# Eleven loads of V issued by GpSimd instead of SyncE, in a cross-covariance attention kernel

## Chip, cores and metric

One core of one Trainium2 chip. The metric is device time in microseconds (us) for one execution of the whole kernel. Beside it stands one execution taken by the hardware profiler; its span runs from the first to the last instruction. The engines are named as in the profile: PE is TensorE (PEld its weight loads), DVE is VectorE, ACT is ScalarE, POOL is GpSimd, SP is SyncE. SPq and POOLq are the instruction streams of SP and POOL that issue DMAs. The 16 DMA engines move the data, whoever issues.

## The reference

```python
batch, heads, seq, dim = 8, 12, 512, 64          # Q, K, V: float32
Q_norm = Q / (np.linalg.norm(Q, axis=-2, keepdims=True) + 1e-10)
K_norm = K / (np.linalg.norm(K, axis=-2, keepdims=True) + 1e-10)
attn = np.einsum('bhnd,bhne->bhde', Q_norm, K_norm)
attn = np.exp(attn - np.max(attn, axis=-1, keepdims=True))
attn = attn / (np.sum(attn, axis=-1, keepdims=True) + 1e-10)
return np.einsum('bhnd,bhde->bhne', V, attn).astype(np.float32)
```

For each of the 96 heads the attention matrix is 64 x 64, over the feature dimension. Each of Q, K, V and the output is 12.58 MB, so 50.3 MB cross the DMA engines.

## The kernel before

**Tiles.** Four heads make a unit `u` (24 of them), two units a stage `s` (12), two stages a group `w` (6). A stage has 1 MB of Q and 1 MB of K; both live in one tile `qk32[s]`, of which there are three buffers. V is loaded per group in two tiles `v32[w, r]` of 1 MB (128 partitions, 8 KB each in one piece), of which there are three buffers too, so the load of one V tile waits until the tile three before it has been read. Q, K and the output go in pieces of 4 KB. Early stages and the last one load Q and K in halves of 512 KB, and the last V tile comes in two halves.

**Work.** For each unit, Q is cast to bf16 by POOL and K by DVE or ACT (`cast_qk`, L212, named cq), DVE makes two masked copies of K (`mask_k`, L222, named mk), ACT squares Q (`square_q`, L228), and PE multiplies (`grams`, L245, and `norms_q`, L253). For each stage there follow the sums and powers that give the norms, the scaling of the 64 x 64 matrices on POOL (`scale_k`, L293, tile kqs), their transposes, the exponentials on ACT (L307) and the normalised bf16 matrix on DVE (L316). V is cast to bf16 (`cast_v`, named cv, tile vb), each half of a tile on POOL or ACT, transposed by PE (L327), copied out of PSUM by ACT (tile vt) and multiplied with the attention matrix (`outs`, L343). DVE copies the result to the output tile `so` (`ocopy`, four copies a stage), and two stores of 512 KB a stage take it to memory. All casts and copies go through one helper and so stand under L172 (ACT), L174 (DVE) or L176 (POOL).

**Order.** The order of instructions is written out by a planner (`Order`). It gives each piece an engine, the pieces it comes after, and a rank, and simulates the pieces with fixed costs; the list of pieces sorted by their planned begin is then emitted, each piece into the instruction stream of its engine, which executes in that order. The loads and stores are pieces of one planned engine, DMA. Which real engine issues a load is decided only in the function that emits it (`load_qk`, `load_v`, `store`); in the kernel before, that is SP for all but the first two loads of K, which ACT issues. A load's place among the other instructions of the issuing engine is that of the planned list. Around the first V loads the list reads, in this order: Q cast of unit 2 (POOL), first V load, Q cast of unit 3 (POOL), second V load, loads of Q and K of stage 4, Q cast of unit 4 and scaling of stage 0 (POOL), third V load, Q cast of unit 5 (POOL). The fourth stands behind POOL's cast of the first V tile, the fifth behind POOL's cast of the second one.

The line that calls the load and gives its waits is L453 in the loop over `w` and `r`: `free` are the casts of the V tile three before, and `last` keeps the V loads in order. Only the last tile is asked for in halves; all eleven others are whole (`c is None`).

Of the kernel before, what the change touches and what calls it, by code (L numbers as in the profile page):

```python
# [111 lines left out]
def kernel(  # L112
# [7 lines left out]
    nc = tc.nc  # L120
# [16 lines left out]
    Vu = V.rearrange("b h (p t) d -> (b h p) (t d)", t=2 * T).rearrange("(w r p) x -> w r p x", r=2, p=128)  # L137
# [55 lines left out]
    def load_v(w, r, c):  # L193
        if (w, r) not in v32:
            v32[w, r] = vp.tile([128, 2, T * D], F32, name="v32")
        o, i = v32[w, r], Vu[w, r].rearrange("p (c x) -> p c x", c=2)
        if c is None:
            nc.sync.dma_start(out=o.rearrange("p c x -> p (c x)"), in_=Vu[w, r])
        else:
            nc.sync.dma_start(out=o[:, c], in_=i[:, c])  # L200

# [220 lines left out]
    for u in range(U):  # L422
        s, r = divmod(u, 2)
# [23 lines left out]
    for w in range(W):  # L447
        for r in range(2):
            halves = (0, 1) if (w, r) == (W - 1, 1) else (None,)
            n = 2 * w + r - NB["v"]  # L450
            for c in halves:
                free = [("cv", n // 2, n % 2, h) for h in range(2)] if n >= 0 else []
                piece(("lv", w, r, c), {"DMA": X if c is not None else 2 * X}, free, [last], v_at(4 * w + 2 * r + (c or 0)), load_v, w, r, c)  # L453
                last = ("lv", w, r, c)
            for c in range(2):
                free = [("vt", w - NB["vb"], *t) for t in turns(w - NB["vb"])] if w >= NB["vb"] else []
                piece(("cv", w, r, c), {"POOL": 1.04, "DVE": (0.62, BIAS["cv"]), "ACT": (0.95, BIAS["ca"])},
                      [("lv", w, r, c if len(halves) == 2 else None)] + free, [("cv", w, r, 0)] if c else [], R["cv"] + 0.01 * (4 * w + 2 * r + c), cast_v, w, r, c)
        for n, (q, f) in enumerate(turns(w)):
            if f is None:  # L460
                before = turns(w)[n - 1] if n else turns(w - 1)[-1] if w else None
                wait = [("vc", w if n else w - 1, *before)] if before else []
            else:
                wait = [("kq", S - 1), ("rd", S - 1)] + ([("vc", w, *turns(w)[n - 4])] if n >= 4 and turns(w)[n - 4][1] is not None else [])
            piece(("vt", w, q, f), {"PE": 0.4 if f is not None else 0.65}, [("cv", w, r, c) for r in range(2) for c in range(2)] + wait, [turned],
                  R["vt"] + 0.02 * w, vtrans, w, q, f)
            turned = ("vt", w, q, f)
            copies = {"ACT": 0.57 if f is not None else 0.97}
            copies["DVE"] = (0.6 if f is not None else 1.12, BIAS["vc"])
            free = [("ou", 2 * (w - NB["vt"]) + e, x) for e in range(2) for x in range(4)] if w >= NB["vt"] else []  # L470
            piece(("vc", w, q, f), copies, [("vt", w, q, f)] + free, [("vc", w, *turns(w)[n - 1])] if n else [], R["vc"] + 0.02 * w, vcopy, w, q, f)
# [57 lines left out]
```

## Time and profile before

| | |
|---|---|
| time, median of 3 runs | 127.59 us (127.54 to 127.77) |
| the profiled execution's span | 125.9 us |
| bytes moved, mean rate over the span | 50.63 MB, 402 GB/s |
| busy: PE | 79.6 us (63%) |
| busy: DVE | 98.8 us (78%) |
| busy: ACT | 91.0 us (72%) |
| busy: POOL | 50.0 us (40%) |
| V loads issued by SP | 11 of 1024 KB, 2 of 512 KB |
| POOL's waits for V to land | 8.2 us, 6 times |
| SP's waits for ACT's cast of V before a V load | 9.9 us, 3 times |
| PE's waits for the masked K (gram matmuls) | 23.3 us, 18 times |

The profiler's page shows each engine's busy time, the span in 40 equal slices with the busy share in tenths, the DMA queues with packets, bytes and share, and groups of instructions by line. Answers of the trace give the same for a stretch of time (busy time by stage), the instructions of one engine in order (timeline: start, length, engine, line, operation, output and input, and in brackets the idle time before with what ended it), and the waits. Queue q1 is the one that SP's DMAs use, q10 that of ACT, q8 the fetching of instructions. A DMA on 16 engines is recorded as packets; their start, length, queue and size are in the trace.

### The profile page before, as it was taken

The numbers are of one execution on the slowest core, as the hardware profiler recorded it, in microseconds if no ns is written. First come the engines' busy times: TensorE is split into PE (matmuls) and PEld (weight loads), VectorE is DVE, ScalarE is ACT, GpSimd is POOL, SyncE is SP. The second block draws the span as 40 slices with busy tenths as digits, with TensorE's granted clock in tenths as the row PEclk, the third lists the DMA queues.
The fourth block names the chain that finished last, engine by engine and source line by source line (L and its number), as shares of the span: only waits on it lengthen the run. The fifth ranks groups of instructions, "written<-read, shape, count | busy, mean of one in ns | idle before, by whom it ended". The sixth has DMA issues, their size and how long they took to land.

```text
span 125.9 us, 4630 instructions
## 1 busy us (share of the span) xinstructions
PE 79.6 (63%) x1944; PEld 63.9 (51%) x1944; DVE 98.8 (78%) x198; ACT 91.0 (72%) x217; POOL 50.0 (40%) x68
## 2 busy tenths in 40 slices
PE   0036949258789857766776668676794875976000
PEld 0035848236668745555665555555683764754000
DVE  3189676967959399987999989999979999999200
ACT  4243476579979999499999999999499997670000
POOL 6243353384561836633437226138743551000000
PEclk9999999955555899999999999999779999599555
DMA  3999999999999999999999999999999999999993
GB/s 105 401 419 419 422 414 418 432 424 410 439 409 418 414 433 414 410 431 419 411 428 428 403 419 423 424 424 407 426 413 420 410 415 407 417 411 404 400 411 134
DMA packets 12159, 50.63 MB, mean 402 GB/s; under 512 B 1130, under 2 KB 1130, under 8 KB 10730
## 3 DMA queue, kind: packets, MB, share of 16 engines
q1 hardware_dynamic: 11850, 49.29, 95.9%
q10 hardware_dynamic: 288, 1.05, 2.1%
q8 instruction: 15, 0.25, 0.7%
q14 instruction: 6, 0.05, 0.1%
HBM read 37.75 MB, written 12.58 MB: 400 GB/s over the span
## 4 chain that ended last, share of the span: by engine, by line
DVE 32%; ACT 24%; DMA 18%; PE 8%; issue 7%; POOL 3%; ACTq 0%; SPq 0%; POOLq 0%
DMA out_dram<-so 12%; DVE so L174 12%; DVE km L222 10%; DMA qk<-in_K_dram 6%; PE gram L245 6%; ACT vt L172 5%; ACT q L228 5%; ACT qkb L172 4%; ACT ex L307 4%; DVE ab L316 4%; DVE qkb L174 3%; ACT vb L172 2%; ACT kq L172 2%; POOL vb L176 2%; DVE n L280 1%
## 5 line engine op out<-in xcount | busy, mean ns | idle before, releaser
L245 PE MATMUL gram<-qkb,km 64*128 64x128 bf16 x768 | 33.3, 252 | 23.3 <-DVE km L222 23.3
L245 PEld LDWEIGHTS <-km 64*128 64x128 bf16 x768 | 28.3, 113 | 26.7 <-DVE km L222 26.3
L176 POOL TENSOR_SCALAR qkb<-qk 128x1024 bf16<-128x1024 f32 x24 | 25.4, 1062 | 28.6 <-PE gram L245 19.9
L222 DVE TENSOR_SCALAR km<-qkb,pick 128x1024 bf16<-128x1024 bf16 x48 | 30.3, 671 | 3.0 <-ACT qkb L172 2.4
L174 DVE COPY so<-po 128x512 f32<-128x512 f32 x48 | 30.8, 684 | 0.4
L228 ACT ACTIVATE q<-qk 128x1024 bf16<-128x1024 f32 x24 | 25.5, 1065 | 6.3 <-DMA qk<-in_Q_dram 4.3
L343 PE MATMUL po<-ab,vt 128*32 128x128 bf16 x768 | 20.1, 231 | 9.5 <-DVE so L174 6.9
L172 ACT COPY vt<-vps 128x1024 bf16<-128x1024 bf16 (+1 forms) x26 | 24.5, 956 | 1.2 <-PE vps L327 1.0
L343 PEld LDWEIGHTS <-vt 128*32 128x32 bf16 x768 | 13.4, 100 | 14.9 <-issue 10.7
L327 PE MATMUL vps<-identb,vb 128*128 128x128 bf16 x192 | 16.7, 237 | 3.0 <-ACT vt L172 2.2
L176 POOL TENSOR_SCALAR vb<-v 128x1024 bf16<-128x1024 f32 x13 | 15.0, 1156 | 8.4 <-DMA v<-in_V_dram 8.2
L307 ACT ACTIVATE ex<-lg,r 128x64 f32<-128x64 f32 x48 | 14.5, 325 | 1.6 <-PE lg L300 1.6
L327 PEld LDWEIGHTS <-vb 128*128 128x128 bf16 x192 | 12.6, 106 | 6.0 <-issue 3.1
L174 DVE CAST qkb<-qk 128x1024 bf16<-128x1024 f32 x13 | 12.1, 933 | 4.2 <-DMA qk<-in_K_dram 4.1
L293 POOL TENSOR_TENSOR kqs<-kq,r 128x256 f32<-128x256 f32 x12 | 7.9, 660 | 18.8 <-ACT r L289 8.3
L316 DVE TENSOR_TENSOR ab<-ex,rinv 64x256 bf16<-64x256 f32 x24 | 12.1, 504 | 0.6
L260 DVE SCALAR_TENSOR_TENSOR scr<-gram,eye 128x256 f32<-128x256 f32 x12 | 5.1, 424 | 8.5 <-ACT kq L172 5.7
L172 ACT CAST vb<-v 128x1024 bf16<-128x1024 f32 x11 | 11.7, 1062 | 0.0
L172 ACT CAST qkb<-qk 128x1024 bf16<-128x1024 f32 x11 | 11.6, 1054 | 0.0
L307 ACT ACTIVATION_READ_ACCUMULATOR ex<-lg,r 128x1 f32 x48 | 10.4, 217 | 0.0
L172 ACT COPY kq<-gram 128x256 f32<-128x256 f32 x12 | 4.6, 380 | 7.1 <-PE gram L253 3.1
L253 PEld LDWEIGHTS <-q 128*128 128x128 bf16 x192 | 7.5, 100 | 3.7 <-issue 2.7
(25 smaller groups left out, 41.1 us busy)
## 6 DMA issues: line engine op xcount, KB each, us to landing
out_dram<-so SPq DMA_DIRECT2D x23, 512.0 KB, 9.8
v<-in_V_dram SPq DMA_DIRECT2D x11, 1024.0 KB, 15.8
qk<-in_Q_dram SPq DMA_DIRECT2D x8, 1024.0 KB, 15.9
qk<-in_K_dram SPq DMA_DIRECT2D x8, 1024.0 KB, 17.6
qk<-in_Q_dram SPq DMA_DIRECT2D x8, 512.0 KB, 8.7
qk<-in_K_dram SPq DMA_DIRECT2D x6, 512.0 KB, 9.6
qk<-in_K_dram ACTq DMA_DIRECT2D x2, 512.0 KB
v<-in_V_dram SPq DMA_DIRECT2D x2, 512.0 KB
```

The costliest lines, as they stand in the source:

```text
L172: nc.scalar.copy(o, i)
L174: nc.vector.tensor_copy(o, i)
L176: nc.gpsimd.tensor_scalar(out=o, in0=i, scalar1=1.0, scalar2=0.0, op0=ALU.mult, op1=ALU.add)
L222: nc.vector.tensor_scalar(out=km[u][:, :, a], in0=qkb[u][:, :, 0], scalar1=pick[:, a:a + 1], scalar2=None, op0=ALU.mult)
L228: nc.scalar.activation(q2[u], qk32[s][:, 0, r], AF.Square)
L245: nc.tensor.matmul(gram[s][:, 2 * g + r, 0:2 * D], km[u][rows, t].rearrange("p a d -> p (a d)"), qkb[u][rows, t].rearrange("p x d -> p (x ...
L253: nc.tensor.matmul(gram[s][:, 0, 2 * D + HU * r:2 * D + HU * (r + 1)], q2[u][:, 2 * t:2 * t + 2].rearrange("p t d -> p (t d)"), heads, sta ...
L293: (nc.vector if eng == "DVE" else nc.gpsimd).tensor_tensor(out=kqs[s], in0=kq[s], in1=r8[s][:, 0:HU, None].to_broadcast([128, 4, D]), op=A ...
L307: nc.scalar.activation(e[:, h, :], lg[s][:, h, :], AF.Exp, scale=r8[s][:, HU + h:HU + h + 1], accum_out=z[:, h:h + 1])
L316: nc.vector.tensor_tensor(out=a[half, :, half], in0=e[half], in1=ri[half, :, None].to_broadcast([D, HU, D]), op=ALU.mult,)
L327: nc.tensor.transpose(ps[:, c, n, :], vb[w][:, J * c + j].rearrange("p r d -> p (r d)"), identb)
L343: nc.tensor.matmul(po[s, x][32 * h:32 * (h + 1), j].rearrange("p r d -> p (r d)"), v, ab[s][:, h, :])
```

## The change

In `load_v` the whole-tile loads of V are issued by `nc.gpsimd` in place of `nc.sync`, with `single_packet=True`: the pieces that one DMA engine moves for a load belong to one packet. The planner, its list, the buffers and the two half loads of the last V tile stay as they are. In the stream of POOL each of the eleven loads takes the place that the planned list gives it.

```diff
             v32[w, r] = vp.tile([128, 2, T * D], F32, name="v32")
         o, i = v32[w, r], Vu[w, r].rearrange("p (c x) -> p c x", c=2)
         if c is None:
-            nc.sync.dma_start(out=o.rearrange("p c x -> p (c x)"), in_=Vu[w, r])
+            nc.gpsimd.dma_start(out=o.rearrange("p c x -> p (c x)"), in_=Vu[w, r], single_packet=True)
         else:
             nc.sync.dma_start(out=o[:, c], in_=i[:, c])
```

## The prediction

> **What bounds the kernel now.** I read the page first: the span, the slices of the DMA engines, the queues.
>
> ```profile
> span 125.9 us, 4630 instructions
> ...
> DMA  3999999999999999999999999999999999999993
> ...
> q1 hardware_dynamic: 11850, 49.29, 95.9%
> q10 hardware_dynamic: 288, 1.05, 2.1%
> ...
> v<-in_V_dram SPq DMA_DIRECT2D x11, 1024.0 KB, 15.8
> ```
>
> From the second slice to the last but one the 16 DMA engines are full. A load of V lands 15.8 us after its issue because it stands in SP's queue behind some 6 MB. So the byte stream is one bound: 50.6 MB at about 0.416 MB per us. The second view is busy time by stage (columns: PE, PEld, DVE, ACT, POOL, then the granted clock, the DMA share, GB/s):
>
> ```profile
> 22.00:46.00 24.00, 16.91 (x293) 13.25 (x291) 18.48 (x37) 20.49 (x52) 12.86 (x13) 0.64 1.02 421
> 46.00:58.00 12.00, 9.11 (x274) 7.54 (x275) 10.70 (x21) 10.34 (x16) 4.99 (x5) 1.00 1.02 420
> 58.00:84.00 26.00, 18.69 (x539) 14.77 (x538) 24.63 (x55) 25.65 (x66) 11.47 (x12) 1.00 1.02 420
> 84.00:118.00 34.00, 24.03 (x648) 18.65 (x645) 31.50 (x61) 24.32 (x66) 11.81 (x12) 0.88 1.02 413
> ```
>
> Until 46 us DVE and ACT have room. After that they have almost none: ACT is busy 25.65 of 26 us, then DVE 31.50 of 34. So compute is a second bound close behind the first, and whatever delays it before 46 us can hardly be made up. The third view is the timeline: the last eleven copies to the output tile end at 110.67+6.69 = 117.36, 8.5 us before the end.
>
> ```profile
> 110.67 6.69 DVE L174 COPY so<-po 128x512 f32<-128x512 f32 x11
> ```
>
> To place each load I laid the trace's packets of SP's queue end to end in the order of issue (1 MB takes 2.5 to 2.6 us). Last packet and first use: K of stage s=2 17.7 and 20.8, Q of s=3 20.2 and 22.1, K of s=3 22.8 and 25.0, K of s=5 40.4 and 43.3, K of s=6 47.8 and 52.3, K of s=7 55.5 and 59.4. A cast starts no sooner than about 1.4 us after the last packet. Compute therefore follows its Q and K with 1 to 3 us to spare.
>
> **The change, part by part.**
>
> *SP.* Eleven issues of 0.34 us go, 3.7 us of SP in all. They lie beside a queue that is some 15 us deep. Worth nothing.
>
> *Bytes.* The same 11 MB move. In the packet records 2, 4 and 8 KB take 84, 159 and 309 ns: 9 ns each, and 300 ns per 8 KB. V has 8 such pieces per engine and load; as one packet it could save 7 x 9 ns, over 11 loads 0.7 us. Bounds: -0.7, and +0.6 if V moves at the pace of the 4 KB loads (2.56 instead of 2.51 us per MB). I take -0.6. It counts only where bytes end last.
>
> *Issue on POOL.* No row shows one. Bounds: 0.34 us as on SP, 1.3 us as the longest Q or V cast beside DVE. I take 1.0, nearest to the usual cast of 1.04 us over the same 128 partitions: 11 us on an engine that is idle for 76. The load also waits in POOL's order for its buffer, freed by the casts of the load three before. The planner's list puts each behind a V cast of POOL, while the other half is often ACT's and later: ACT's ends at 40.3 where POOL's ended at 38.1, 48.2 against 45.7, 56.1 against 53.0. POOL stands for 2 to 3 us, then issues. Behind it stands the next Q cast (47.22 would become some 49.2, 55.58 some 57.1), and the gram matmuls wait for that. The K cast of the same unit is later still (52.3, 59.4), so I cost this at nothing; without that cover it is 1.5 to 2 us a time.
>
> *Order of arrival.* This decides. V leaves SP's queue and no longer stands behind 15 us of other loads. What two queues do to each other is seen at the start, where the two K loads on ACT's queue run beside SP's (window 3 to 7 us):
>
> ```profile
> q1 hardware_dynamic: 214, 0.81, 52.9%
> q10 hardware_dynamic: 215, 0.82, 50.1%
> ```
>
> Equal packets, equal shares: the engines alternate. A V packet of 64 KB against one of 4 KB then takes nearly the whole engine for 2.5 us. The Trainium skill ("DMA: Bandwidth & Descriptors", queues, rings and completion order) says the engine changes rings only at packet boundaries; the rows agree for 4 KB, none shows 64 KB. By equal shares of bytes instead V would need 5 us, still far sooner than now, and the same bytes would be ahead of Q and K.
>
> When is V issued? POOL's timeline early on:
>
> ```profile
> 10.33 1.04 POOL L176 TENSOR_SCALAR qkb<-qk 128x1024 bf16<-128x1024 f32 x1 [0.97 <-PE gram L245]
> 13.75 1.04 POOL L176 TENSOR_SCALAR qkb<-qk 128x1024 bf16<-128x1024 f32 x1 [2.38 <-PE gram L245]
> 15.88 1.04 POOL L176 TENSOR_SCALAR qkb<-qk 128x1024 bf16<-128x1024 f32 x1 [1.09 <-PE gram L245]
> 17.59 0.61 POOL L293 TENSOR_TENSOR kqs<-kq,r 128x256 f32<-128x256 f32 x1 [0.67 <-ACT r L289]
> ```
>
> The first load stands behind the cast at 10.33, the second behind that at 13.75, the third behind the kqs at 17.59. With 1 us of issue their bytes run at about 12.4, 15.8 and, with its predecessors pushed back, 22.6; now they run at 22.5, 24.9 and 32.5. So Q and K of s=2 and s=3 come 2.5 to 7.5 us later: K of s=3 at 30.3 instead of 22.8, its cast at 31.7 instead of 25.0. Later each V passes about two stages of Q or K. Following the queue by hand, K of s=5 lands at 45.5 and is cast at 46.9 instead of 43.3: **+3.6 us**. For s=6 and s=7 the same 5 us minus spare give +2.3.
>
> What is regained: from 46 to 84 us ACT is idle 2.0 us and DVE 2.7; I let 1.2 us of that go. From 84 to 117.36 DVE is idle 1.9 us; I let 0.9 go. Leaves +1.5 at the last copy.
>
> *DVE beside POOL.* Two mk operations take 0.88 us undisturbed and 1.53 to 1.72 beside a POOL cast. If writing descriptors disturbs them as a cast does, an issue costs up to 0.65 us when it meets one; casts to qkb and mk fill 42.4 of 125.9 us, a third. Of 11 issues 7 come after 44 us: 7 x 0.65 = 4.5 at most, 0 at least, 1.5 with one in three. I take 1.5. **Compute ends 3.0 us later**, bounds 0 and 6.
>
> *V sooner.* POOL now waits 8.2 us for V in all. ACT's half of each V is cast 2 to 5 us after landing, hence not limited by it, and the transposes need both halves. Gain: nothing.
>
> *The end.* Stage 9's copies end at 112.5 and its store's packets begin at 115.95; 1.0 us lies between an issue and its first packet (0.75 and 1.76 at the start). So 2.4 us of lateness hide behind stored-up stores (stage 11: 117.36 and 121.17, 2.8 us). The byte saving does not count then, since compute ends last. **Sum: +3.0 - 2.4 = +0.6 us** on the span of 125.9, 126.5. The median of the runs shown, 127.59, stands 1.7 us above the span; I carry that over: 128.2.
>
> **Rivals.**
>
> *Only issue time moves, or less than 2 us of lateness remains (faster).* Then the stores cover all and the 0.6 us of packet overhead come off: 127.0. For it: DMA is busy to the end and compute ends 8.5 us before it. The Trainium skill ("DMA: Bandwidth & Descriptors", issuing engines are not separate DMA queues) says that issuing from several engines saves only sequencer time; that would leave 127.6, as SP's 3.7 us lie beside a full queue, and speaks against the change. Without the saving per packet and with the lateness hidden, the rows give 127.6 too: the same bytes through engines that are full either way. Against both: Q and K have only 1 to 3 us to spare. Faster 0.30; no change, 127.4 to 127.8, 0.14.
>
> *POOL blocks (slower, more).* POOL stands in front of ACT's V cast, and the Q casts and kqs behind it become the wait of the grams. Price: at 31, 40, 48 and 56 us 1.5, 0.7, 2.0 and 1.5 us, 5.7 in all, half of it covered by the K casts: +2.9 on top of the lateness that already fills the cover, giving about 130.5, up to 131. It decides once an issue takes over some 1.5 us, or POOL ends after the K cast. For it: POOL's kqs at 61.54 and 66.88 are in the chain that ended last. Against: POOL is idle 60% of the time. Chance 0.20.
>
> *The forecast,* +0.2 to +1.8 us: 0.36.
>
> **How the numbers follow.** What can be told from no change is 0.2%, about 0.25 us. Likeliest: 128.2, own range 127.8 to 129.4. The range for 8 in 10 takes in the faster case down to 126.8 and most of POOL's blocking: 126.8 to 130.6. Faster 0.30, same 0.14, slower 0.36 + 0.20 = 0.56.
>
> **What would show it.** A POOL issue of about 1 us; V landing 3 to 6 us after its issue instead of 15.8; the first three V loads done before 26 us; PE waiting longer for mk before 46 us (23.3 us of the gram's waits now); the last copy at about 120.4; the DMA slices below 9 in the last six. Wrong: if the last copy stays within 2 us of 117.36, the forecast falls to the faster case; if V lands as late as now, nothing was passed and the order argument is void; if POOL's waits for ACT's V cast end the grams' waits, it is the blocking case.

## The result, and the profile after

The changed kernel takes **137.22 us** (median of 4 runs, 135.59 to 138.06) against 127.62 us (127.54 to 127.77) beside it: slower by 9.6 us. The ratio, 1.066 (95% interval 1.061 to 1.071), is that of the two fast executions, 135.59 and 136.65 us (spans of 133.8 and 134.9 us); the profiled one below is a slow one, 137.79 us with a span of 136.0, so 1 to 2 us of the lateness read from it may be its own. The forecast was 128.2 us, at most 130.6.

From the page of the changed kernel: the span, the slices of the DMA engines, the queues (packets, MB, share), POOL's issues and one group of DVE (count, then busy us and mean ns), and the V loads with their time from issue to landing.

```profile
span 136.0 us, 4627 instructions
...
DMA  3999999999999999999999999999779998757792
...
q1 hardware_dynamic: 10266, 37.75, 70.1%
q0 software_dynamic: 1584, 11.54, 20.8%
...
L316 DVE TENSOR_TENSOR ab<-ex,rinv 64x256 bf16<-64x256 f32 x24 | 16.1, 669 | 0.6
...
L198 POOL DMA_DIRECT2D v<-in_V_dram x11 | 6.8, 617 | 17.6 <-ACT vb L172 8.4
...
v<-in_V_dram POOLq DMA_DIRECT2D x11, 1024.0 KB, 9.5
```

V now comes by a queue of its own, q0, and lands 9.5 us after its issue in place of 15.8. The DMA engines, full to the last slice but one before, run partly dry twice: at 97 to 102 us and from 114 us on. The byte stream no longer sets the end; compute does. The busy time by stage of the changed kernel (columns as in the prediction):

```profile
22.00:46.00 24.00, 12.07 (x196) 9.82 (x196) 15.26 (x34) 14.90 (x36) 10.56 (x11) 0.60 1.02 420
46.00:58.00 12.00, 7.19 (x206) 5.98 (x203) 9.79 (x14) 9.37 (x22) 7.97 (x10) 0.93 1.01 416
58.00:84.00 26.00, 18.55 (x462) 14.93 (x461) 23.41 (x48) 22.72 (x53) 10.64 (x13) 0.83 1.02 405
84.00:118.00 34.00, 25.20 (x664) 20.66 (x664) 29.21 (x62) 29.48 (x73) 15.52 (x17) 0.89 0.92 357
```

In the first row ACT does 14.90 us of work where it did 20.49: that is where the time begins to go. The timeline of DVE in the changed kernel (start, length, engine, line), at the K cast that was forecast for 31.7 us and at the last copies, with the same K cast of before ahead of them:

```profile
25.02 0.69 DVE L174 CAST qkb<-qk 128x1024 bf16<-128x1024 f32 x1
```

```profile
31.80 0.94 DVE L174 CAST qkb<-qk 128x1024 bf16<-128x1024 f32 x1 [5.54 <-DMA qk<-in_K_dram]
...
121.67 6.69 DVE L174 COPY so<-po 128x512 f32<-128x512 f32 x11
```

The cast stood at 25.02 before. The last copies end at 121.67 + 6.69 = 128.36, 11.0 us after the 117.36 of before. From there to the end of the span there are 7.6 us instead of 8.5, so 0.9 us of the lateness is hidden: 11.0 - 0.9 = 10.1 us, the whole difference of the spans.

To see where lateness arises, the table gives the starts of five of DVE's twelve row reductions (`n<-scr`, one for each stage's norms) and the end of the last copy, each less that of before, in us, read from DVE's timelines. The rows below the first are the experiments. Even in a kernel that takes the same time as before such starts differ by up to 2.2 us (third row).

| kernel | 3rd (28.6) | 5th (47.1) | 6th (58.4) | 8th (72.2) | 12th (104.6) | last copy (117.4) |
|---|---|---|---|---|---|---|
| the change | +5.6 | +5.8 | +9.0 | +10.3 | +11.0 | +11.0 |
| e1: first three loads by POOL, others by SP | +5.7 | +5.4 | +5.4 | +6.2 | +7.4 | +7.8 |
| e10: POOL only stands, V by SP | -0.6 | -2.2 | -1.4 | -1.0 | +0.2 | +0.2 |
| e7: SP issues all, first three V early | +5.8 | +5.5 | +5.5 | +6.2 | +7.4 | +7.3 |
| e18: e7 with less work for ACT | +5.7 | +6.4 | +6.9 | +7.7 | +8.1 | +8.3 |
| e13: e7, and POOL stands | +6.0 | +5.3 | +5.4 | +6.5 | +5.6 | +6.4 |
| e16: e13, and POOL issues eight small DMAs | +6.0 | +7.2 | +8.0 | +9.9 | +10.2 | +10.9 |
| e17: e10, and POOL issues eight small DMAs | -1.5 | -1.2 | +1.2 | +2.5 | +3.5 | +3.5 |

The change shows two steps: +5.6 by 28.6 us, and from 47 us on another 5.2.

### The profile page after: what moved, and what is told of

Its sections match the earlier page's. It is cut to its first block, busy times and chain, and to the rows that moved or that the text cites. A ratio compares the mean times of both kernels' runs of the same rounds, so it can differ in the third digit from the quotient of the medians.

```text
span 136.0 us, 4627 instructions
## 1 busy us (share of the span) xinstructions
PE 80.8 (59%) x1944; PEld 65.7 (48%) x1944; DVE 100.4 (74%) x198; ACT 91.5 (67%) x217; POOL 55.7 (41%) x79
## 4 chain that ended last, share of the span: by engine, by line
DVE 34%; DMA 33%; ACT 10%; PE 7%; issue 4%; POOL 3%; SPq 1%; POOLq 0%; ACTq 0%; DVEq 0%
DMA qk<-in_K_dram 22%; DVE so L174 14%; DMA out_dram<-so 12%; DVE ab L316 7%; DVE km L222 6%; PE gram L245 4%; DVE qkb L174 3%; ACT ex L307 3%; POOL qkb L176 2%; ACT vb L172 2%; ACT vt L172 2%; ACT qkb L172 2%; PE po L343 2%; PE vps L327 1%; DVE scr L260 1%
## 5 line engine op out<-in xcount | busy, mean ns | idle before, releaser
L245 PE MATMUL gram<-qkb,km 64*128 64x128 bf16 x768 | 35.2, 262 | 25.1 <-DVE km L222 25.0
L245 PEld LDWEIGHTS <-km 64*128 64x128 bf16 x768 | 30.1, 118 | 28.3 <-DVE km L222 27.8
L222 DVE TENSOR_SCALAR km<-qkb,pick 128x1024 bf16<-128x1024 bf16 x48 | 26.4, 591 | 2.9 <-ACT qkb L172 2.3
L174 DVE CAST qkb<-qk 128x1024 bf16<-128x1024 f32 x13 | 13.2, 1018 | 12.6 <-DMA qk<-in_K_dram 12.5
L327 PE MATMUL vps<-identb,vb 128*128 128x128 bf16 x192 | 16.9, 239 | 3.0 <-ACT vt L172 2.9
L316 DVE TENSOR_TENSOR ab<-ex,rinv 64x256 bf16<-64x256 f32 x24 | 16.1, 669 | 0.6
L198 POOL DMA_DIRECT2D v<-in_V_dram x11 | 6.8, 617 | 17.6 <-ACT vb L172 8.4
L307 ACT ACTIVATION_READ_ACCUMULATOR ex<-lg,r 128x1 f32 x48 | 10.3, 214 | 0.0
```

What stands on the lines that cost most here:

```text
L174: nc.vector.tensor_copy(o, i)
L198: nc.gpsimd.dma_start(out=o.rearrange("p c x -> p (c x)"), in_=Vu[w, r], single_packet=True)
L222: nc.vector.tensor_scalar(out=km[u][:, :, a], in0=qkb[u][:, :, 0], scalar1=pick[:, a:a + 1], scalar2=None, op0=ALU.mult)
L245: nc.tensor.matmul(gram[s][:, 2 * g + r, 0:2 * D], km[u][rows, t].rearrange("p a d -> p (a d)"), qkb[u][rows, t].rearrange("p x d -> p (x ...
L307: nc.scalar.activation(e[:, h, :], lg[s][:, h, :], AF.Exp, scale=r8[s][:, HU + h:HU + h + 1], accum_out=z[:, h:h + 1])
L316: nc.vector.tensor_tensor(out=a[half, :, half], in0=e[half], in1=ri[half, :, None].to_broadcast([D, HU, D]), op=ALU.mult,)
```

## The experiments

### The first step: which loads are late, and who issues them

**e1** leaves only the first three loads to POOL.

```diff
-            nc.gpsimd.dma_start(out=o.rearrange("p c x -> p (c x)"), in_=Vu[w, r], single_packet=True)
+            if 2 * w + r < 3:
+                nc.gpsimd.dma_start(out=o.rearrange("p c x -> p (c x)"), in_=Vu[w, r], single_packet=True)
+            else:
+                nc.sync.dma_start(out=o.rearrange("p c x -> p (c x)"), in_=Vu[w, r])
```

> Only the first three loads of V are issued by POOL, the other eight by SP as before. Theory A (order of arrival: the three loads pass Q and K of stages 2 and 3, and compute never makes it up): K of stage 3 lands at about 30 us as after the change (22.8 before), the cast of it comes some 7 us late, the lateness from 35 us on stays at 5 to 6 us, and the last copy of the output comes 5 to 6 us after 117.4. With 2.4 to 2.8 us hidden behind stored-up stores that is +2.5 to +3.5 us: 130 to 131.2. Theory B (POOL's stream: it stands before a V load for ACT's cast, and its backlog then holds DVE off): these three loads wait for no buffer, so nothing of it is here: 127.4 to 128.2.

133.9 us (133.05 to 135.62), ratio 1.045 (1.040 to 1.051). Three issues make over two thirds of the loss, more than the 130 to 131.2 us expected.

**e2** is the complement (`>= 3`).

> The first three loads of V are issued by SP, the other eight by POOL. Theory A: the early lateness is gone; later V loads still pass 2 to 2.5 us of Q and K, which leaves 0 to 1.5 us of lateness, hidden behind the stores: 127.2 to 128.2. Theory B: POOL stands for ACT's V cast before at least four of the loads, its next casts run back to back, and at least one DVE instruction of L316 is drawn out to over 2 us (4.1 us after the change); lateness grows by the 3.6 and 2 us that were seen at 55 to 61 and 84 to 90 us: 130 to 132. Both together would be about additive with the first run.

133.29 us, ratio 1.042 (1.037 to 1.046): a miss for every theory that gave these loads next to nothing. Compute is on time to 36 us. Then K of stage 5 lands at 46.0 instead of 40.3, its cast is 5.7 us late, and the lateness is +4.6 at the fifth reduction and +6.7 at the last copy. So the first load that overtakes Q and K makes the kernel late, whichever it is, and the losses of e1 and e2 don't add up: a later load does no second harm to a stage that is late already. Part of the loss of e2 is not order: POOL also issues eight loads in it, which has a price of its own (the second step below).

**e7** takes POOL out of it: the kernel before, with SP issuing everything, but Q and K of stages 3 and 4 put behind the first three V loads on SP's queue.

```diff
+    moved = {
+        ('lq', 3, None): ('lv', 1, 0, None),
+        ('lk', 3, None): ('lv', 1, 0, None),
+        ('lq', 4, None): ('lv', 1, 0, None),
+        ('lk', 4, None): ('lv', 1, 0, None),
+    }
...
+        if key in moved:
+            waiting.setdefault(moved[key], []).append(emit)
+            continue
```

> SP issues every load, as before the change; only the order on SP's queue differs: the first three loads of V stand ahead of Q and K of stage 3 (Q and K of stages 3 and 4 behind them). POOL issues nothing. Theory A: K of stage 3 lands at about 30 us, its cast comes 7 us late, 5 to 6 us of lateness stay to the end as in the run with three loads on POOL: 131.5 to 134. If instead the descriptors made by POOL or the second queue were what costs, this one is 127.4 to 129.

133.98 us (133.02 to 134.02), ratio 1.047 (1.043 to 1.051), the same as e1. The same K cast in the timeline of DVE in e7:

```profile
31.80 1.14 DVE L174 CAST qkb<-qk 128x1024 bf16<-128x1024 f32 x1 [8.36 <-DMA qk<-in_K_dram]
```

It starts at 31.80, to the hundredth as in the changed kernel, and no DMA is POOL's. The first step is the order of arrival. The granted clock is no part of it: in e7 it was 1.0 up to 73 us, 0.937 over the span (0.870 before).

**e4, e9, e11** let POOL issue later. In e4 the first three loads stand further back in POOL's stream (behind the scaling of stage 0 and the Q casts of units 5 and 7), in e9 all eleven do, each shortly before it is needed; in e11 SP issues the first three and POOL the eight others late. The edit is a `moved` list as in e7, with the V loads as keys, for example `('lv', 0, 0, None): ('sc', 0)`.

> All eleven loads on POOL, but the first three stand later in POOL's stream: the first behind the scaling of stage 0, the second behind the Q cast of unit 5, the third behind that of unit 7. Theory A: Q and K of stages 2 and 3 land as before the change to within 3 us, the 5 to 6 us of lateness by 35 us shrink to under 3, and the time falls by 3 us or more, to 129.5 to 133. Theory B: the first three loads hold nobody, so moving them changes nothing: 135.5 to 138.

> All eleven loads on POOL, each so late in POOL's stream that V should land about when it did before the change (issue 7 to 10 us ahead). Theory A: Q and K land within 1.5 us of before, lateness at the last copy under 2 us: 127.3 to 129. If the cost is in the issue by POOL itself (descriptors, the second queue), 131 or more stays.

> SP issues the first three loads of V in their old order; POOL issues the other eight, each so late in its stream that V should land about when it did before. Theory A (only the order of arrival counts): Q and K land within 2 us of before and mostly within 1, lateness at the last copy under 2 us: 127.3 to 128.8. If issue by POOL costs by itself (descriptors, second queue, 0.6 us on POOL each), lateness grows with each load and 130 or more comes out, as with the eight loads at their old places (1.042).

| | time, us | ratio (95%) | last copy |
|---|---|---|---|
| e4 | 131.77 (131.05 to 133.55) | 1.029 (1.024 to 1.034) | +5.0 |
| e9 | 131.47 (131.18 to 131.74) | 1.028 (1.027 to 1.030) | +4.9 |
| e11 | 129.59 (128.85 to 129.92) | 1.013 (1.008 to 1.018) | +3.3 |

The later V comes in, the less is lost, but none reaches the time before; e9 and e11 missed the 129 and 128.8 us that the order of arrival was to allow at most. Two reasons are seen. In e9 K of stage 3 still lands 4.7 us late, since the two loads of V that it meets take 4.0 and 5.0 us from first packet to last. And DVE is held beside POOL after an issue, in a K cast of 2.44 us in e9 and 2.18 us in e11, which is the subject of the second step. No version beat the kernel before.

### Why nothing is regained

In e7 Q and K of later stages land as before and then wait 6 us and more for their casts. Yet lateness is 5.8 at the third reduction and 5.5 at the seventh.

**e12** gives e7 three buffers of the bf16 Q, K tile and of masked K instead of two.

```diff
-    qkp = ctx.enter_context(tc.tile_pool(name="qkp", bufs=NB["qkb"]))
-    kmp = ctx.enter_context(tc.tile_pool(name="kmp", bufs=NB["km"]))
+    qkp = ctx.enter_context(tc.tile_pool(name="qkp", bufs=3))
+    kmp = ctx.enter_context(tc.tile_pool(name="kmp", bufs=3))
```

> As the run e7_sp_first3 (SP issues all, the first three loads of V ahead of stage 3), but the bf16 tiles of Q and K and the masked copies of K have three buffers and not two; the order of instructions is the same. It asks why 5.8 us of lateness stay although Q and K then wait 6 us and more for their casts. If the two buffers set the pace from 30 us on, lateness shrinks from 5.8 to under 4 by 60 us: 130 to 132.5. If the fixed order of the instructions on DVE and ACT does, it stays: 133 to 134.2.

134.0 us, ratio 1.049 (1.044 to 1.053), and lateness is +6.4 at the fifth reduction: the buffers are not the reason. A small gain could be hidden, since the new buffers also move other tiles (see e8).

**e18 and e19.** The busy times of e7 pointed to ACT. For units 8 to 11 ACT squares only 2 of 16 rows of each partition (so these norms are left incomplete), in e7 (e18) and, as a control, in the kernel before (e19).

```diff
     def square_q(u):
...
+        if 8 <= u < 12:
+            nc.scalar.activation(q2[u][:, 0:2], qk32[s][:, 0, r][:, 0:2], AF.Square)
+            return
         nc.scalar.activation(q2[u], qk32[s][:, 0, r], AF.Square)
```

> The kernel in which SP issues all, the first three loads of V ahead of Q and K of stages 3 and 4 (133.98 us, compute 5.5 to 5.8 us late from 30 to 66 us), with less work for ACT: for units 8 to 11 ACT squares only the first 2 of 16 rows of Q for each partition, and the norm matmuls of these units read those rows only, so the norms of four units are not the reference's. In the run without this edit these four squares stand between 40 and 50.6 us; ACT has about 0.85 us less to do in each, 3.4 us in all. Theory ACT (from about 30 us on ACT has no room, 17.20 us busy of 18.10, so lateness can't be regained): the start of the fifth row reduction of the norms comes 2.5 to 4 us sooner than there, lateness 2 to 3 us in place of 5.5, and stays so; the time 130.5 to 132.3 us. Theory of another pace (DVE, PE, POOL, the order of arrival or the buffers): lateness stays 5 to 5.8 us, time 133.3 to 134.2 us.

> The same four short squares in the kernel before, as the control. Both theories: the loads arrive as before and the 16 DMA engines are full to the end, so 127.3 to 127.8 us, ratio 0.997 to 1.001, compute at most 3 us sooner at the fifth row reduction.

e18: 134.1 us (133.77 to 135.87), ratio 1.047 (1.043 to 1.052). e19: 127.66 us, 0.999 (0.997 to 1.001). The theory of a full ACT falls. The stretch 34.4 to 52.5 us, first in e7, then in e18 (columns as above; ACT, the fourth engine, has 17.20 and 13.88 us):

```profile
34.40:52.50 18.10, 14.99 (x280) 12.02 (x283) 13.79 (x28) 17.20 (x41) 9.36 (x9) 1.00 1.02 420
```

```profile
34.40:52.50 18.10, 13.33 (x248) 10.52 (x250) 13.99 (x27) 13.88 (x41) 9.56 (x9) 0.69 1.02 420
```

ACT has 3.3 us less to do, and not more gets done. The two traces were not taken at one clock (0.69 and 1.00 in this stretch), so a slower PE in e18 could hide a gain. Other executions of e18 had 0.83 to 0.91 over the span and took 133.8 to 134.3 us, others of e7 0.83 to 0.90 and 133.0 to 134.0 us: no gain there either. What sets the pace instead is seen in the chain of waits of e18, in order of time (start, length, what):

```profile
39.24 1.91 PE gram L248 x32
...
41.23 0.38 ACT kq L172
...
41.63 0.04 DVE scr L263
...
41.97 1.01 DVE qkb L174
43.01 1.53 DVE km L222 x2
...
45.84 2.06 DVE km L222 x2
...
47.94 1.09 PE gram L248 x32
```

The chain goes round: PE's grams, ACT's copy of them, DVE's `scr`, the K cast that stands behind `scr` in DVE's written order, the masked K, and PE's grams again: 8.7 us from grams to grams, with each engine waiting for the last one. That this round trip sets the pace is read from this chain; a kernel with the K cast ahead of `scr` was not tried, so it is not shown that this would regain anything. One pair of masks ran beside a POOL cast in e18 and not in e7 (2.04 us, 0.88 in e7).

What the traces do show is that compute had a pace of its own before the change too. These are all the waits of the compute engines for a load in the kernel before, from 24 to 118 us (total, times, longest):

```profile
POOL vb L176 <- DMA v<-in_V_dram: 8.2, 6, 2.2
...
POOL qkb L176 <- DMA qk<-in_Q_dram: 0.3, 1, 0.3
```

DVE and ACT never wait for Q or K there. From the third row reduction to the twelfth compute takes 75.9 us before and 77.5 us in e7, 8.4 and 8.6 us a stage. Loads that came a few us too late stopped it once, and loads that are early again afterwards could not make it go faster.

### The packet

**e3** drops `single_packet=True` from the change.

> All eleven loads on POOL, without the request for one packet for each engine. In the trace of the changed kernel V's 8 KB pieces and the 4 KB pieces of SP's queue share the engines about 2 to 1 by bytes and every V piece takes 309 ns, as if each piece were a packet of its own. If so, nothing changes: 135.5 to 138. If the request does give V a larger share, V's loads get slower without it (3.8 us for the first now), Q and K of stages 2 and 3 arrive earlier by up to 2 us, and the time falls to 134 to 135.

137.7 us (136.94 to 138.92), ratio 1.077 (1.068 to 1.085), its interval overlapping that of the change. In the trace's packets V goes in the same 8 KB pieces of 309 ns in both, and while V runs it takes two thirds of the bytes (568 KB against 236 KB in 2 us), as if engines took one 8 KB piece of q0 and one 4 KB piece of q1 in turn. No effect of the single packet shows. The Trainium skill ("DMA: Bandwidth & Descriptors", Queues, rings and completion order) lets an engine change queues at packet boundaries only; if that holds, the 64 KB were never one packet here.

### The second step: POOL's standing, or its issuing

The second step starts in the changed kernel at 54 us. The timeline of POOL there:

```profile
54.22 0.60 POOL L198 DMA_DIRECT2D v<-in_V_dram  x1 [3.94 <-ACT r L289]
54.85 1.06 POOL L176 TENSOR_SCALAR qkb<-qk 128x1024 bf16<-128x1024 f32 x1
55.86 0.62 POOL L293 TENSOR_TENSOR kqs<-kq,r 128x256 f32<-128x256 f32 x1
56.45 1.04 POOL L176 TENSOR_SCALAR qkb<-qk 128x1024 bf16<-128x1024 f32 x1
57.46 1.03 POOL L176 TENSOR_SCALAR vb<-v 128x1024 bf16<-128x1024 f32 x1
```

and of DVE:

```profile
54.65 4.55 DVE L316 TENSOR_TENSOR ab<-ex,rinv 64x256 bf16<-64x256 f32 x2
```

A pair of L316 takes 0.85 us undisturbed. Here it lasts from 54.65 to 59.20 (one of the two 4.12 us), until 0.7 us after POOL's run of four has ended. In e7 the same pair runs from 54.53 to 55.59 us. So the change, after six issues, is 0.1 us behind e7 when this pair begins, and 3.6 us behind when it ends; at the last copy it is 3.7. In e3 the hold comes again at the same place (4.19 us at 54.88).

**e5** moves six later loads back in POOL's stream, so that POOL never stands for ACT's V cast; the first three are as in the change.

> All eleven loads on POOL, the first three where the change has them; six of the others stand one or more POOL instructions later, where ACT's cast of the buffer's old tile is done by the plan. Theory A (order of arrival): the early lateness of 5 to 6 us stays. Theory B (POOL stands and its backlog holds DVE off) adds the step of 3.6 us at 55 to 61 us in the changed kernel: without the standing it should go, no L316 over 2 us, lateness 5.5 to 7.5 at the end, 131.5 to 134. If the step is still there, it is not POOL's standing: 135.5 to 138.

136.2 us (135.81 to 137.28), ratio 1.068 (1.062 to 1.072): as the change, and in the range that was to mean that POOL's standing is not the cause. The step at 54 us is gone (+6.5 at the sixth reduction), but an L316 of 2.50 us follows beside another run behind an issue, at 75.4 us, and lateness ends at 9.0. Where POOL issues these six does not matter much.

**e8 and e10** test the standing by itself: SP issues V as before, and at eight places POOL copies two elements of the bf16 V tile that the load would have waited for.

```diff
+            n = 2 * w + r - NB["v"]
+            if n >= 0:
+                nc.gpsimd.tensor_copy(pad[:, 0:2], vb[n // 2][:, 0:T + 1:T, n % 2, 0:1].rearrange("p c o -> p (c o)"))
             nc.sync.dma_start(out=o.rearrange("p c x -> p (c x)"), in_=Vu[w, r])
```

In e8 the copy goes to a new tile of 4 bytes a partition, in e10 to the tile `pad` that exists.

> SP issues every load, as before the change. At the eight later places where the change has a V load in POOL's stream, POOL copies two elements of the bf16 tile that the casts of the old V tile wrote, so POOL stands there until ACT's cast is done and issues nothing. Theory B alone: backlog on POOL and DVE held off beside it, lateness of 1 to 4 us from about 50 us on: 128 to 131. Theory A: nothing passes anything, within 0.5 us of before: 127.4 to 128.2.

> As the run e8_stand (SP issues all loads; POOL stands for ACT's V cast at the eight later places), but the two elements go into a tile that is there already, so no tile moves: in e8_stand a new tile of 4 bytes a partition shifted the tiles behind it and the 4 KB packets took 162.7 ns on average instead of 160.8. If the standing itself cost the 2 us, this one is 129.2 to 130 again; if the shifted tiles did, 127.4 to 128.2.

e8: 129.71 us, ratio 1.016 (1.014 to 1.017). e10: 127.64 us (10 runs), 0.999 (0.997 to 1.001). Standing costs nothing; the new tile costs 1.6% (more below).

**e13** has the standing of e10 in e7, where compute is late.

> The runs e7_sp_first3 and e10_stand in one: SP issues all loads, the first three of V ahead of stage 3 (5.8 us of lateness), and POOL stands for ACT's V cast at the eight later places and issues nothing. The change costs 6.6%, the early order alone 4.7%, the standing alone nothing. If standing costs once compute is late (POOL then has its next instructions ready, runs them back to back and holds DVE off), one L316 is drawn out to over 2 us and the time is 135 to 137, as after the change. If the rest of the change's cost comes from POOL's issue of the eight loads itself, this one is 133 to 134.2, as e7_sp_first3.

132.94 us, ratio 1.042 (1.036 to 1.048): nothing there either.

**e14 and e15** add to e13 and e10 a DMA by POOL at the same eight places, 4 bytes for each of 128 partitions; V still comes by SP.

```diff
             if n >= 0:
...
+                nc.gpsimd.dma_start(out=pad[:, 2:3], in_=Vu[w, r][:, 0:1])
```

> As the run e13_late_stand (5.8 us late by the order of loads on SP, POOL standing at eight places), and POOL now also issues a DMA of 4 bytes a partition at each of the eight places; V itself still comes by SP. The change costs 6.6%, the early order alone 4.2 to 4.7%. If what is left (about 2%) is the making of descriptors by POOL while compute is late, an L316 of over 2 us shows again and the time is 135 to 137. If it is the 1 MB of V on a second queue, this stays at 132.5 to 134.

> The same eight small DMAs by POOL, with the loads in the order of before, so that compute is on time. If an issue by POOL costs DVE something whether late or not, lateness of 1 to 3 us and 128.2 to 130; if it costs only when compute is late, or never, 127.4 to 128.1.

e14: 137.7 us, 1.077 (1.073 to 1.080). e15: 129.34 us, 1.010 (1.007 to 1.013). That is the price of issuing (e14 0.7 us above the range given), but the sign named for it is missing in e14: no L316 is over 1.2 us, it is a K cast of DVE that takes 3.66 us (3.51 in e15). And all eight write one column, so POOL also waited for each to land (4.8 us, 3 times, in e15), and the cause stayed open. **e16 and e17** are the same with a column for each.

```diff
-                nc.gpsimd.dma_start(out=pad[:, 2:3], in_=Vu[w, r][:, 0:1])
+                nc.gpsimd.dma_start(out=pad[:, 2 + 2 * w + r:3 + 2 * w + r], in_=Vu[w, r][:, 0:1])
```

> As the kernel with a small DMA by POOL at each of the eight places of the loads in time (129.34 us, ratio 1.0098), but each small DMA writes a column of its own, so that POOL no longer waits for the one before it to land. If the 1.0% came from these waits for landing: 127.4 to 127.9 us, ratio 0.998 to 1.002, and no DVE instruction above 1.5 us. If it comes from issuing on POOL as such: 128.7 to 129.6 us, ratio 1.008 to 1.015, and a DVE instruction of 2.5 us or more beside a run of POOL's instructions that follows an issue.

> The same columns of their own in the kernel that is made late by SP's order (132.94 us without the small DMAs, 137.7 us with them in one column). If the 3.5% came from POOL's waits for landing: 132.5 to 133.6 us, ratio 1.038 to 1.047. If it comes from issuing on POOL as such: 136 to 138 us, ratio 1.066 to 1.08.

e17: 130.11 us (129.64 to 130.48), **1.019 (1.017 to 1.021)**, against 0.999 of e10. e16: 136.44 us (135.41 to 137.52), **1.066 (1.063 to 1.069)**, against 1.042 of e13. It is the issuing, and in e17 it costs more than the 128.7 to 129.6 us expected. The queue of these eight DMAs on the page of e17 shows that it is not their bytes:

```profile
q0 software_dynamic: 256, 0.00, 0.2%
```

What it does is seen at one place where e10 and e17 run the same instructions within 0.8 us of each other. POOL and then DVE in e10:

```profile
47.36 1.04 POOL L176 TENSOR_SCALAR qkb<-qk 128x1024 bf16<-128x1024 f32 x1
48.37 0.77 POOL L296 TENSOR_TENSOR kqs<-kq,r 128x256 f32<-128x256 f32 x1
49.11 1.04 POOL L176 TENSOR_SCALAR qkb<-qk 128x1024 bf16<-128x1024 f32 x1
...
46.93 1.74 DVE L319 TENSOR_TENSOR ab<-ex,rinv 64x256 bf16<-64x256 f32 x2
```

and in e17:

```profile
47.53 0.58 POOL L201 DMA_DIRECT2D pad<-in_V_dram  x1
48.15 1.06 POOL L176 TENSOR_SCALAR qkb<-qk 128x1024 bf16<-128x1024 f32 x1
49.17 0.62 POOL L297 TENSOR_TENSOR kqs<-kq,r 128x256 f32<-128x256 f32 x1
49.75 1.04 POOL L176 TENSOR_SCALAR qkb<-qk 128x1024 bf16<-128x1024 f32 x1
...
47.62 3.45 DVE L320 TENSOR_TENSOR ab<-ex,rinv 64x256 bf16<-64x256 f32 x2
```

In e10 DVE gets in between POOL's instructions: the pair ends at 48.67, after POOL's first, and POOL's `kqs` is the one that gives way (0.77 us). In e17 POOL's three run undisturbed to 50.79 and DVE's pair ends at 51.07. The longest single one of these (L316, L319 or L320, by the lines added) is 1.31 us in e10, 3.02 in e17, 4.12 in the change and 1.20 before. In e16 it is other DVE instructions that are held: a K cast of 2.56 us, a pair of masks of 2.70. Most issues are followed by no such hold: in e17 only two of the eight are followed by a DVE instruction of 2 us or more. Order (4.7 points of the ratio in e7) and issuing (2.0 and 2.4 points) together make 6.7 to 7.1, against 6.6 of the change.

## Why the prediction was wrong

**The order of arrival, as events: right for stage 3, wrong for stage 5.** Forecast for stage 3 were K at 30.3 and, by the same 7.5 us, Q at 27.7; the packets show 30.1 and 27.5. The cast was forecast for 31.7 and came at 31.80. POOL's first issues begin at 11.39, 13.76 and 17.28 us, the first V packet 3.9 us behind the first. K of s=5, forecast for 45.5, landed at 41.0 (40.35 before), because POOL came to the fourth V load only at 36.07 us. It decided nothing: that stage was late already.

**"What is regained ... Leaves +1.5 at the last copy": the step that failed.** The prediction had +6.7 us in hand at the K cast of stage 3, then went on with the +3.6 of stage 5 and +2.3 of stages 6 and 7, as if compute returned to its loads in between, and let 2.1 us more go. Measured with the order alone (e7): +5.5 at the seventh reduction and +7.3 at the last copy. The stage busy times were read as room ("until 46 us DVE and ACT have room"). The waits of before show no stretch after 24 us in which DVE or ACT waited for Q or K, so there was none in which earlier loads could have helped; and in e18 work taken off ACT was not replaced by other work. This term was off by 5.8 us of the 9.5 that the spans are apart (126.5 and 136.0); the next two terms make 2.2 and 1.5.

**"DVE beside POOL ... I take 1.5": right in kind, too small.** The issues cost +4.5 at the last copy where compute is late (e16 against e13) and +3.3 where it is on time (e17 against e10), 2.4 and 2.0 points of the ratio; in the change what stands beyond e7 is 3.7. (The profiled executions of e16 and of the change took 1.1 and 0.6 us more than their medians.) The bound of 0.65 us an issue was that of one POOL cast; after some issues DVE was held for several POOL instructions.

The Trainium skill ("SBUF — State Buffer", SBUF: two separate sides) says that a DVE operation with two inputs in SBUF and a GpSimd operation that reads SBUF exclude each other on a shared port, and that whichever starts first keeps it for its whole instruction. The 1.31 us of L319 in e10 agrees, as a hold behind one POOL instruction; the 3.02 us in e17, behind three in a row, goes beyond it. Why an issue makes POOL's next instructions keep DVE out is not shown here.

**"2.4 us hide behind stored-up stores": 0.9.** From the last copy to the end of the span it was 8.5 us before, 7.6 in the change, 7.4 in e7 and e11. About 1 us hides, whether compute is 3.3 or 11 us late. SP's own waits in the changed kernel (total, times, longest) show what came of the stored-up work:

```profile
SPq L210 <- DVE so L174: 17.7, 4, 8.0
SPq L200 <- ACT vb L172: 12.0, 1, 12.0
```

SP stands 12.0 us for ACT's V cast at a half load of the last V tile, with the stores behind it, and then for DVE's output copies: the DMA engines run partly dry before the end, and little is left to hide behind.

**Bytes -0.6: not there**, by e3 and the packets (V still goes in recorded pieces of 8 KB), and it would not have counted. **SP worth nothing: right.** **POOL's issue: 0.62 us, not 1.0**; what it costs is not its own length.

**The signs named in advance.** V after 3 to 6 us: 9.5. The first three V done before 26 us: 19.4, 23.2 and 28.0. PE's wait for masked K before 46 us: 18.1 us against 16.9, hardly longer, though compute was 5.8 us late. Last copy at 120.4: 128.36. Slices below 9 at the end: five of the last six.

**The rivals.** "POOL blocks" named the standing: POOL did stand 8.4 us for ACT's V cast, and by e10 and e13 it costs nothing. The rule of the Trainium skill ("DMA: Bandwidth & Descriptors", Issuing engines are not separate DMA queues) that another issuing engine saves sequencer time only would have given no change. The runs differ from it: three loads by another engine cost 4.5% in e1, which e7 shows to be the order of arrival (4.7% with SP alone), and in e17 issuing alone costs 1.9%. The faster case needed less than 2 us of lateness; there were 11.

## What to carry to other kernels

Moving a load to another issuing engine moves it to another queue, past all that was ahead of it: write down what it overtakes and when that is needed, and carry the lateness of the first overtaken load to the end, unless the chain of waits shows a stretch where compute truly waits for its loads. Idle time of engines is no proof of such a stretch. GpSimd's issue can have a price beyond its length where VectorE runs beside it (here 2.0 points of the ratio for eight), and it can be measured alone with small DMAs.

## What was not expected of the hardware

- Behind some DMA issues on POOL of about 0.6 us, also such that move 512 bytes (e14 to e17), DVE instructions are held to 2.0 to 4.1 us, over up to four POOL instructions. In the kernels in which POOL issues nothing the longest L316 was 1.2 to 1.3 us, and the longest DVE instruction of any kind between 6 and 105 us was 1.55.
- A new tile of 4 bytes a partition, which shifts the tiles behind it, made the kernel 1.6% slower (e8 against e10). SP's 4 KB packets took 162.7 ns on average instead of 160.6, the 8 KB ones 315.6 instead of 309.4; that the shift is the cause is not shown. Experiments that add a tile need a control.
- A single packet was asked for each engine, 64 KB of V, and V still shared the engines with SP's queue in pieces of 8 KB (568 KB against 236 KB in 2 us).
- The granted clock of TensorE ran from 0.78 to 0.94 over the profiled spans without an order in the times: 0.791 in e10 at 127.61 us, 0.937 in e7 at 133.95.
